# Joints of an eight-norm trunk in float32: six output tiles side by side, and VectorE alone for the sums

## The chip, the core and the metric

The kernel runs on one core of a Trainium2 chip. The metric is the device time of one execution in microseconds (us); lower is better. The engines are TensorE (PE, the matrix products; PEld its weight loads), VectorE (DVE), ScalarE (ACT), GpSimd (POOL) and SyncE (SP, which issues the weight loads).

## What is computed

A trunk of two layers on 272 tokens (16 learned ones and 256 of the input) by 1024 features, all in float32. Each layer has three sublayers: a feed-forward part, a mixer (a gated short convolution in layer 0, differential attention with 8 heads in layer 1), and a second feed-forward part. Each sublayer is normed on its way in and on its way out:

```python
def rms_norm(t, g, eps=1e-6):
    return t * rsqrt(mean(t * t, axis=-1) + eps) * g

def swiglu(h, w_gu, w_down):                     # 1024 -> 2 x 2816 -> 1024
    g, u = split(h @ w_gu, 2, axis=-1)
    return (silu(g) * u) @ w_down

for i in range(2):
    f = swiglu(rms_norm(h, ln_ffn1[i, 0]), ffn1_w_gu[i], ffn1_w_down[i])
    h = h + 0.5 * rms_norm(f, ln_ffn1[i, 1])
    m = mixer(rms_norm(h, ln_mix[i, 0]))         # 1024 -> 3072 -> 1024
    h = h + rms_norm(m, ln_mix[i, 1])
    f = swiglu(rms_norm(h, ln_ffn2[i, 0]), ffn2_w_gu[i], ffn2_w_down[i])
    h = h + 0.5 * rms_norm(f, ln_ffn2[i, 1])
return h[:, 16:]
```

## The kernel before

Activations lie transposed, 128 features by 272 tokens a tile, eight tiles (k = 0 to 7) for 1024 features. From the attention's queries on, 256 tokens are enough. Every weight tile of 128x128 and every activation tile is split into two float32r parts, hi and lo, that add up to it: ScalarE casts the upper part (L138, L212) and VectorE subtracts (L140, L213). A product is then three matmuls: hi by hi, hi by lo of x, lo by hi (`mm3`, L164 to L166).

Weights come as loads of 1 MB with 16 tiles each into three buffers. `prepare` splits a *group* of 8 tiles into one of `HIS = 7` pairs of buffers, about four groups ahead of TensorE; it does so when the program comes to certain tiles of the stream. TensorE's instructions have the order of the program; those of the other engines are ordered by a scheduler.

The sublayers are called f0, cv (convolution), f1, f2, at (attention) and f3. Between one's last down-projection tile and the next one's up-projection lies a *joint*:

- `Post.root`: the mean of the squares of the eight output tiles, as matmuls with a matrix of ones (`ms_out`, L287), the root on ScalarE (`sz`, L313), and ten products that nothing reads (`warm_a`, `warm_b`).
- `Pre.first`: x for k = 0. The residual h and the output f have been multiplied by the gain on GpSimd; VectorE then does hg * s (L379) and the sum, written as x's upper part (L380); GpSimd does the same sum in full (L381), and VectorE takes the lower part from it (L384).
- `Post.z` for k = 1 to 7 on VectorE: t = h * s (L321), z = t + f (L323); `split` with the gain: ScalarE hi (L212), VectorE lo (L213).
- the squares of z on ScalarE (`sq_in`), summed up on GpSimd (`acc_in`, L271).

Since a projection is linear, the norm ahead of it is not applied to x; its factor is put on the output. So TensorE can start on k = 0 at once: `order_up` takes the first `KO = 4` output tiles k by k, tiles 0 to 31 in the order of use, and all others one after the other. At tile `LATE = 40` the mean `ms_in` is formed, from the sum split into hi and lo; then come root and reciprocal (`rs`), and only then are output tiles taken from their PSUM banks, of which there are eight. At this place the residual is brought back, too: h = z / s, a reciprocal on VectorE (`rho`, L330) and eight products on GpSimd (L334).

In attention, the rotation of q and k ends on GpSimd (`rot_q`, `rot_k`, `q`, `k`, L529 and L530), and head 0's scores are put ahead of tile 62 or later (`t0 + 6`), each further part of a head at its own tile.

The functions that the change touches, with the lines of the profile:

## Time and profile before

| | |
|---|---|
| median of 3 runs | 1080.92 us (1080.53 to 1081.65) |
| the profiled execution's span (its own time, first to last instruction) | 1078.5 us |
| PE busy | 1042.0 us, 97% |
| DVE / ACT / POOL busy | 739.5 / 562.5 / 273.0 us |
| weights and inputs read | 174.08 MB, 162 GB/s over the span |

The median is 2.4 us above the span of the profiled execution; no row shows what lies in between. Matmuls are pipelined, so the 0.29 us of a matmul's record are no step; the step is the distance between two starts. A row gives its start, its duration, engine, line, tiles written and read, and in brackets the idle time ahead of it and what ended it. L numbers are lines of the kernel before.

### The profile page before, as it was taken

Reading aid. Unit: us, or ns where it says so; the run is one execution under the profiler, and the core shown is the slowest. Engines: PE = TensorE matmul, PEld = TensorE weight load, DVE = VectorE, ACT = ScalarE, POOL = GpSimd, SP = SyncE. Lnnn points to the kernel's source line nnn. Section 1 sums busy time; section 2 is a strip of 40 time slices with the busy share of each in tenths; the row PEclk is TensorE's granted clock in tenths of the full one; section 3 lists DMA queues with packets and bytes.
Section 4 is the critical chain, followed back from the end, with each engine's and each line's share of the span. In section 5 each row is a group of like instructions: output and inputs, shape, how many; then the busy total and the mean of one; then the engine's idle time right before and its main releaser. Section 6 shows DMA issues by size and latency. Waiting matters only on the chain.

```text
span 1078.5 us, 20013 instructions
## 1 busy us (share of the span) xinstructions
PE 1042.0 (97%) x7948; PEld 1009.6 (94%) x7948; DVE 739.5 (69%) x1379; ACT 562.5 (52%) x1231; POOL 273.0 (25%) x285
## 2 busy tenths in 40 slices
PE   8999999999999999999899999998899989999997
PEld 7999999899989999999799999997889979999986
DVE  6966654498749966644598665438999879866543
ACT  7744444355546644445366444445466656655542
POOL 4211110161137211110363111105612135211000
PEclk9999999999999999999999999999899999999999
DMA  7755445326532754444137545450344413745541
GB/s 272 260 192 174 179 171 182 118 79 234 196 118 78 261 189 176 171 182 160 75 123 274 191 162 191 157 195 5 114 157 157 153 43 131 286 177 190 176 156 40
DMA packets 26878, 176.41 MB, mean 164 GB/s; under 512 B 3104, under 2 KB 4256, under 8 KB 6048
## 3 DMA queue, kind: packets, MB, share of 16 engines
q1 hardware_dynamic: 26640, 175.08, 45.1%
q8 instruction: 62, 1.02, 0.4%
q14 instruction: 32, 0.26, 0.1%
q10 hardware_dynamic: 144, 0.06, 0.0%
HBM read 174.08 MB, written 1.05 MB: 162 GB/s over the span
## 4 chain that ended last, share of the span: by engine, by line
PE 83%; DVE 11%; issue 2%; ACT 2%; POOL 1%; DMA 0%; SPq 0%; DVEq 0%; POOLq 0%
PE ps_guf L166 14%; PE ps_guf L164 14%; PE ps_guf L165 14%; PE ps_dnf L164 6%; PE ps_dnf L166 6%; PE ps_dnf L165 6%; PE ps_cin L166 2%; PE ps_out L697 2%; PE ps_out L695 2%; PE ps_out L696 2%; PE ps_cin L165 2%; PE ps_cin L164 2%; DVE lo_guf L140 1%; PE ps_qkv L164 1%; PE ps_qkv L166 1%
## 5 line engine op out<-in xcount | busy, mean ns | idle before, releaser
L165 PE MATMUL ps_guf<-x_f_lo,hi_guf 128*128 128x272 f32 (+1 forms) x1392 | 400.2, 288 | 4.3 <-DVE x_f_lo L213 4.3
L164 PE MATMUL ps_guf<-x_f_hi,hi_guf 128*128 128x272 f32 (+1 forms) x1392 | 400.7, 288 | 1.7 <-ACT hi_guf L138 1.7
L166 PE MATMUL ps_guf<-x_f_hi,lo_guf 128*128 128x272 f32 (+1 forms) x1392 | 401.1, 288 | 1.1 <-DVE lo_guf L140 1.1
L138 ACT CAST hi_guf<-raw_guf 128x512 fp32r<-128x512 f32 x352 | 199.6, 617 | 142.6 <-PE ps_guf L165 65.4
L165 PEld LDWEIGHTS ps_guf<-x_f_lo,hi_guf 128*128 128x128 f32 x1392 | 265.3, 191 | 5.3 <-DVE x_f_lo L213 4.9
L164 PEld LDWEIGHTS ps_guf<-x_f_hi,hi_guf 128*128 128x128 f32 x1392 | 263.4, 189 | 2.0 <-ACT hi_guf L138 1.9
L166 PEld LDWEIGHTS ps_guf<-x_f_hi,lo_guf 128*128 128x128 f32 x1392 | 263.0, 189 | 1.7 <-DVE lo_guf L140 1.7
L140 DVE TENSOR_TENSOR lo_guf<-raw_guf,hi_guf 128x512 fp32r<-128x512 f32 x352 | 243.8, 733 | 27.0 <-ACT hi_guf L138 19.7
L423 POOL TENSOR_TENSOR sg_f<-sg_f,rs_f 128x272 f32<-128x272 f32 (+1 forms) x88 | 95.8, 1092 | 356.9 <-ACT sg_f L422 356.8
L140 DVE TENSOR_TENSOR lo_dnf<-raw_dnf,hi_dnf 128x512 fp32r<-128x512 f32 x176 | 114.8, 692 | 101.5 <-ACT hi_dnf L138 99.1
L138 ACT CAST hi_dnf<-raw_dnf 128x512 fp32r<-128x512 f32 x176 | 100.8, 619 | 129.5 <-PE ps_dnf L165 50.6
L164 PE MATMUL ps_dnf<-a_f_hi,hi_dnf 128*128 128x272 f32 x528 | 152.2, 288 | 0.0
L166 PE MATMUL ps_dnf<-a_f_hi,lo_dnf 128*128 128x272 f32 x528 | 152.1, 288 | 0.0
L165 PE MATMUL ps_dnf<-a_f_lo,hi_dnf 128*128 128x272 f32 x528 | 151.7, 287 | 0.0
L165 PEld LDWEIGHTS ps_dnf<-a_f_lo,hi_dnf 128*128 128x128 f32 x528 | 100.0, 189 | 0.0
L164 PEld LDWEIGHTS ps_dnf<-a_f_hi,hi_dnf 128*128 128x128 f32 x528 | 99.4, 188 | 0.0
L166 PEld LDWEIGHTS ps_dnf<-a_f_hi,lo_dnf 128*128 128x128 f32 x528 | 99.2, 188 | 0.0
L428 DVE TENSOR_TENSOR av_f<-ps_guf,sg_f 128x272 f32<-128x272 f32 (+1 forms) x88 | 38.3, 436 | 75.7 <-PE ps_guf L166 61.7
L420 DVE TENSOR_TENSOR g_f<-ps_guf,rs_f 128x272 f32<-128x272 f32 (+1 forms) x88 | 37.4, 432 | 39.1 <-PE ps_guf L166 39.1
L271 POOL TENSOR_TENSOR acc_out_f<-acc_out_f,sq_out_f 128x272 f32<-128x272 f32 x21 | 18.0, 859 | 159.3 <-ACT sq_out_f L269 159.3
L166 PE MATMUL ps_qkv<-x_at_hi,lo_qkv 128*128 128x272 f32 (+1 forms) x188 | 55.3, 294 | 3.0 <-DVE lo_qkv L140 3.0
L164 PE MATMUL ps_qkv<-x_at_hi,hi_qkv 128*128 128x272 f32 (+1 forms) x188 | 57.2, 304 | 0.0
(303 smaller groups left out, 1725.4 us busy)
## 6 DMA issues: line engine op xcount, KB each, us to landing
raw_guf<-in_guf SPq DMA_DIRECT2D x86, 1024.0 KB, 4.8
raw_dnf<-in_dnf SPq DMA_DIRECT2D x44, 1024.0 KB, 4.8
raw_cin<-in_cin SPq DMA_DIRECT2D x12, 1024.0 KB, 4.8
raw_qkv<-in_qkv SPq DMA_DIRECT2D x12, 1024.0 KB, 4.8
raw_cout<-in_cout SPq DMA_DIRECT2D x4, 1024.0 KB, 4.8
raw_o<-in_o SPq DMA_DIRECT2D x4, 1024.0 KB, 4.8
raw_guf<-in_guf SPq DMA_DIRECT2D x8, 256.0 KB, 4.9
h<-in_xT SPq DMA_DIRECT2D x8, 136.0 KB, 4.7
```

The costliest lines, as they stand in the source:

```text
L138: nc.scalar.copy(hi[:, sl], both[:, sl])
L140: nc.vector.tensor_tensor(lo[:, sl], both[:, sl], hi.bitcast(F32)[:, sl], ALU.subtract)
L164: nc.tensor.matmul(o, whi, xhi, start=start, stop=False)
L165: nc.tensor.matmul(o, whi, xlo, start=False, stop=False)
L166: nc.tensor.matmul(o, wlo, xhi, start=False, stop=stop)
L271: self.eng.tensor_tensor(self.acc[:, :n], self.acc[:, :n], sq[:, :n], ALU.add)
L420: nc.vector.tensor_tensor(g[:, :n], p, pre.r, ALU.mult)
L423: nc.gpsimd.tensor_tensor(s[:, :n], s[:, :n], pre.r, ALU.mult)
L428: nc.vector.tensor_tensor(v[:, :n], p, keep.pop(j)[:, :n], ALU.mult)
L695: nc.tensor.matmul(o, xhi[:, tok], whi[:, col], start=k == 0, stop=False)
L696: nc.tensor.matmul(o, xhi[:, tok], wlo[:, col], start=False, stop=False)
L697: nc.tensor.matmul(o, xlo[:, tok], whi[:, col], start=False, stop=k == KF - 1)
```

## The change

`KO` is six and `LATE` is 50: six output tiles run k by k (tiles 0 to 47). In each of these eight k steps TensorE does all six hi-by-hi products first, then the six with the weights' lower part, then the six with x's lower part; before, only k = 0 was done so. GpSimd has no instruction in a joint: VectorE does t, z, x's lower part and the sum of the squares for each k. For k = 0 the gain is put into the first six weight tiles instead of into x (`GAINS`), so that z itself goes to TensorE. The orders of VectorE and ScalarE in the joint are those of the program. The mean `ms_in` is one float32 matmul on the sum. Groups are prepared at k = 2, 6 and 7 of a joint, and two more of them in the last 16 tiles of the stream ahead, so that all seven buffers are filled when a joint begins. The residual h is formed at tile 74 instead of 40, and the attention's heads are 10 tiles later at most. At the start (f0, without a joint) the weights come in pieces of six tiles, VectorE does the sum, and the root's table is loaded first.

```diff
-LATE_AT = (30, 34)
+MORE_AT = (2, 6, 7)
+FIRST_AT = (0, 1, 3, 4, 5, 7)
...
-KO = 4
-LATE = KO * KD + 8
+KO = 6
+LATE = KO * KD + 2
...
+        gain = GAINS[label][:, 0:1] if label in LATER and c == g == 0 else None
+        for s, e in ((0, 4), (4, 8)) if gain is None else ((0, KO), (KO, HC)):
+            sl = slice(s * P, e * P)
+            if gain is None or s:
+                with queued(last["sqrt"]):
+                    nc.scalar.copy(hi[:, sl], both[:, sl])
+                with queued(last["rs"]):
+                    nc.vector.tensor_tensor(lo[:, sl], both[:, sl], hi.bitcast(F32)[:, sl], ALU.subtract)
+            else:
+                nc.scalar.activation(hi[:, sl], both[:, sl], AF.Copy, scale=gain)
+                nc.vector.scalar_tensor_tensor(lo[:, sl], both[:, sl], gain, hi.bitcast(F32)[:, sl], ALU.mult, ALU.subtract)
...
+            if pre is not None:
+                pre.before(i)
+            if label in (*LATER, "guf0") and i <= LATE:
+                pass
+            elif j == HC // 2:
                 prepare()
...
+            elif j == 2 and (i > len(order) - 2 * HC and after.get(label) in LATER or ahead(label, i) < AHEAD):
                 prepare()
             hi, lo = group(label, i)
...
+            xhi, xlo = pre.x0 if pre is not None and i < KO else xs[k]
             x0 = c0 if xhi.shape[1] == T else 0
             args = open_[m][:, :n], whi, wlo, xhi[:, x0 : x0 + n], xlo[:, x0 : x0 + n], count[m] == 0, count[m] == nk - 1
-            if before is None or i >= KO:
+            if pre is None or i >= KO * KD:
                 mm3(*args)
             else:
                 held.append(args)
-                if i == KO - 1:
-                    for o, hi, lo, xhi, xlo, start, _ in held:
+                if len(held) == KO:
+                    for o, hi, lo, xhi, xlo, start, stop in held:
                         nc.tensor.matmul(o, hi, xhi, start=start, stop=False)
-                    for o, hi, lo, xhi, xlo, start, _ in held:
+                    for o, hi, lo, xhi, xlo, start, stop in held:
                         nc.tensor.matmul(o, lo, xhi, start=False, stop=False)
-                    for o, hi, lo, xhi, xlo, start, _ in held:
-                        nc.tensor.matmul(o, hi, xlo, start=False, stop=False)
+                    for o, hi, lo, xhi, xlo, start, stop in held:
+                        nc.tensor.matmul(o, hi, xlo, start=False, stop=stop)
+                    held.clear()
...
+            if self.extra is not None and self.i == 1:
+                nc.vector.scalar_tensor_tensor(self.acc[:, :n], self.extra, EPS * D / P, sq[:, :n], ALU.mult, ALU.add)
+            elif self.i < KD or not self.soon:
                 self.eng.tensor_tensor(self.acc[:, :n], self.acc[:, :n], sq[:, :n], ALU.add)
             else:
                 self.last = sq
...
+            parts = [self.acc, self.last] if self.soon else [self.acc]
+            for i, t in enumerate(parts):
+                nc.tensor.matmul(o, ones, t[:, :n], start=i == 0, stop=i == len(parts) - 1)
...
+        def z(self, hk, k, hi=None):
             n = self.n
             t = tmp.tile([P, T], F32, tag="t", bufs=3, name=f"t_{self.name}_{k}")
-            with queued(self.after):
-                nc.vector.tensor_tensor(t[:, :n], hk[:, self.c0 - (T - hk.shape[1]) :], self.s[:, :n], ALU.mult)
+            nc.vector.tensor_tensor(t[:, :n], hk[:, self.c0 - (T - hk.shape[1]) :], self.s[:, :n], ALU.mult)
             z = self.f[k]
-            self.after = nc.vector.tensor_tensor(z, t[:, :n], self.f[k], ALU.add)
+            if hi is not None:
+                nc.vector.tensor_tensor(hi, t[:, :n], z, ALU.add)
+            nc.vector.tensor_tensor(z, t[:, :n], z, ALU.add)
             return z
...
+            k, j = divmod(i, KO)
+            if i < KD * KO and j == 0:
+                if k == 0:
+                    self.order = ExitStack()
+                    self.order.enter_context(tc.manual_schedule(engines={mybir.EngineType.DVE, mybir.EngineType.Activation}))
+                if self.post is None:
+                    if k == 0:
+                        self.zs = self.hs
+                        self.norm = Norm(f"in_{self.name}", self.n, eng=nc.vector, soon=False)
+                        for e in range(2):
+                            self.part(e)
+                            prepare()
+                        self.x0 = self.xs[0]
+                    if k + 2 < KD:
+                        self.part(k + 2)
+                    if k in FIRST_AT:
+                        prepare()
+                    self.norm.add(self.zs[k])
+                else:
+                    if k == 0:
+                        self.first()
+                        self.step(1)
+                    if k < KD - 1:
+                        self.step(k + 2)
+                    for _ in range(MORE_AT.count(k)):
+                        prepare()
             if i == LATE:
                 self.ms = self.norm.mean()
                 self.ready()
+                self.order.close()
+            if i == LATE + 3 * KD:
+                self.residual()
+            self.parts(i)
...
+            n, post = self.n, self.post
             post.root()
...
+            hi = tmp.tile([P, n], F32R, tag="zh0", bufs=1, name=f"z_{self.name}_0_hi")
+            lo = tmp.tile([P, n], F32R, tag="zl0", bufs=1, name=f"z_{self.name}_0_lo")
+            z = self.zs[0] = post.z(self.hs[0], 0, hi)
+            nc.vector.tensor_tensor(lo, z, hi.bitcast(F32), ALU.subtract)
+            self.x0 = hi, lo
+            self.zs[1] = post.z(self.hs[1], 1)
+            self.norm = Norm(f"in_{self.name}", n, post.ms, nc.vector, soon=False)
+        def step(self, k):
+            if k + 1 < KD:
+                self.zs[k + 1] = self.post.z(self.hs[k + 1], k + 1)
+            if k < KD:
+                self.part(k)
+            if k == KD:
+                self.norm.add(self.zs[k - 1])
+                self.part(0)
+            else:
+                self.norm.add(self.zs[k - 1])
...
-            t0 = max(3 * KD * (hd + 1), 56 + 10 * hd)
+            t0 = max(3 * KD * (hd + 1), LATE + 16 + 10 * hd)
```

How the instructions move, at three places. ScalarE at the end of f0's down projection and the begin of the joint to cv, first before, then after; `sq_out_f` is the square of an output tile, `hi_cin` a group's upper part (x2: two halves), `sz_f` the root:

```order
L138 CAST hi_cin_1_2598<-raw_cin_2566 128x512 x2
L269 ACTIVATE sq_out_f_7_2524<-ps_dnf_6_2443 128x272
L304 ACTIVATE f_f_6_2527<-ps_dnf_6_2443,half_112 128x272
L269 ACTIVATE sq_out_f_8_2616<-ps_dnf_7_2529 128x272
L304 ACTIVATE f_f_7_2618<-ps_dnf_7_2529,half_112 128x272
L313 ACTIVATE sz_f_2634<-ms_out_f_2631 128x272
```

```order
L289 ACTIVATE sq_out_f_7_2529<-ps_dnf_6_2448 128x272
L319 ACTIVATE f_f_6_2532<-ps_dnf_6_2448,half_115 128x272
L144 CAST hi_cin_0_2581<-raw_cin_2579 128x512 x2
L144 CAST hi_cin_1_2605<-raw_cin_2579 128x512 x2
L144 CAST hi_cin_0_2619<-raw_cin_2617 128x512 x2
L289 ACTIVATE sq_out_f_8_2637<-ps_dnf_7_2534 128x272
L319 ACTIVATE f_f_7_2639<-ps_dnf_7_2534,half_115 128x272
L328 ACTIVATE sz_f_2650<-ms_out_f_2647 128x272
```

Three groups more stand between the last square but one and the last; the third takes the seventh pair of buffers. VectorE from the root on in the same joint, before and after:

```order
L379 TENSOR_TENSOR hg_cv<-hg_cv,sz_f_2634 128x272
L380 TENSOR_TENSOR x_cv_hi<-hg_cv,fg_cv 128x272
L321 TENSOR_TENSOR t_f_1_2648<-h_79,sz_f_2634 128x272
L323 TENSOR_TENSOR f_f_1_2068<-t_f_1_2648,f_f_1_2068 128x272
L384 TENSOR_TENSOR x_cv_lo<-x_cv,x_cv_hi 128x272
L321 TENSOR_TENSOR t_f_2_2687<-h_80,sz_f_2634 128x272
L213 SCALAR_TENSOR_TENSOR x_cv_lo<-f_f_1_2068,gains,x_cv_hi 128x272
L323 TENSOR_TENSOR f_f_2_2160<-t_f_2_2687,f_f_2_2160 128x272
```

```order
L334 TENSOR_TENSOR t_f_0_2663<-h_78,sz_f_2650 128x272
L337 TENSOR_TENSOR z_cv_hi<-t_f_0_2663,f_f_0_1987 128x272
L338 TENSOR_TENSOR f_f_0_1987<-t_f_0_2663,f_f_0_1987 128x272
L411 TENSOR_TENSOR z_cv_lo<-f_f_0_1987,z_cv_hi 128x272
L334 TENSOR_TENSOR t_f_1_2668<-h_79,sz_f_2650 128x272
L338 TENSOR_TENSOR f_f_1_2073<-t_f_1_2668,f_f_1_2073 128x272
L334 TENSOR_TENSOR t_f_2_2672<-h_80,sz_f_2650 128x272
L338 TENSOR_TENSOR f_f_2_2167<-t_f_2_2672,f_f_2_2167 128x272
L231 SCALAR_TENSOR_TENSOR x_cv_lo<-f_f_1_2073,gains,x_cv_hi 128x272
L291 SCALAR_TENSOR_TENSOR acc_in_cv<-ms_out_f_2647,sq_in_cv_2679 128x272
```

The full sum of k = 0 is now VectorE's, its lower part comes right after it, and each k ends with a sum of squares. GpSimd in attention, from the residual to head 1's q, before and after (`h_f` is the residual; in each list the first `rot_q`, `rot_k`, `q`, `k` are head 0's):

```order
L334 TENSOR_TENSOR h_f_6_9275<-f_f_6_8864,rho_f_9261 128x272
L334 TENSOR_TENSOR h_f_7_9277<-f_f_7_8957,rho_f_9261 128x272
L376 TENSOR_SCALAR hg_f_10855<-h_f_0_9263,gains 128x256
L529 TENSOR_TENSOR rot_q_9283<-rot_q_9283,sr 128x256
L529 TENSOR_TENSOR rot_k_9289<-rot_k_9289,sr 128x272
L529 TENSOR_TENSOR rot_q_9297<-rot_q_9297,sr 128x256
L530 TENSOR_TENSOR q_9285<-q_9285,rot_q_9283 128x256
L530 TENSOR_TENSOR k_9291<-k_9291,rot_k_9289 128x272
```

```order
L349 TENSOR_TENSOR h_f_3_9483<-f_f_3_8600,rho_f_9475 128x272
L562 TENSOR_TENSOR rot_q_9299<-rot_q_9299,sr 128x256
L562 TENSOR_TENSOR rot_k_9305<-rot_k_9305,sr 128x272
L563 TENSOR_TENSOR q_9301<-q_9301,rot_q_9299 128x256
L562 TENSOR_TENSOR rot_q_9313<-rot_q_9313,sr 128x256
L349 TENSOR_TENSOR h_f_4_9485<-f_f_4_8694,rho_f_9475 128x272
L563 TENSOR_TENSOR k_9307<-k_9307,rot_k_9305 128x272
L349 TENSOR_TENSOR h_f_5_9487<-f_f_5_8780,rho_f_9475 128x272
L349 TENSOR_TENSOR h_f_6_9489<-f_f_6_8873,rho_f_9475 128x272
L349 TENSOR_TENSOR h_f_7_9491<-f_f_7_8980,rho_f_9475 128x272
L563 TENSOR_TENSOR q_9315<-q_9315,rot_q_9313 128x256
```

The residual's eight products, which were all done before the first rotation, now lie among those of heads 0 and 1.

## Rows read from the trace of the kernel before

**Rows 1.** The page: busy time of TensorE, and the chain that ended last, by engine.

```profile
PE 1042.0 (97%) x7948; PEld 1009.6 (94%) x7948; DVE 739.5 (69%) x1379; ACT 562.5 (52%) x1231; POOL 273.0 (25%) x285
PE 83%; DVE 11%; issue 2%; ACT 2%; POOL 1%; DMA 0%; SPq 0%; DVEq 0%; POOLq 0%
```

**Rows 2.** Timeline (start, duration, instruction, idle before) of TensorE, joint f0 to cv.

```profile
208.14 0.29 PE L166 MATMUL ps_dnf<-a_f_hi,lo_dnf 128*128 128x272 f32 x1
...
211.80 0.77 PE L190 MATMUL ps_cin<-x_cv_hi,hi_cin 128*128 128x272 f32 x4 [1.22 <-DVE x_cv_hi L380]
...
214.01 0.77 PE L194 MATMUL ps_cin<-x_cv_lo,hi_cin 128*128 128x272 f32 x4 [0.93 <-DVE x_cv_lo L384]
...
221.68 0.39 PE L165 MATMUL ps_cin<-x_cv_lo,hi_cin 128*128 128x272 f32 x1 [1.81 <-DVE x_cv_lo L213]
...
232.52 0.29 PE L164 MATMUL ps_cin<-x_cv_hi,hi_cin 128*128 128x272 f32 x1
```

**Rows 3.** Stretches (length, busy per engine, PEclk, DMA): joints (f1's left out), half clock, steady work.

```profile
208.14:232.52 24.38, 20.41 (x139) 18.84 (x138) 21.91 (x32) 13.94 (x31) 14.83 (x17) 0.93 0.02 4
...
522.75:547.12 24.37, 19.11 (x139) 17.35 (x138) 21.89 (x32) 13.94 (x31) 14.81 (x17) 1.00 0.03 4
730.65:755.00 24.35, 20.35 (x139) 18.54 (x138) 21.90 (x36) 13.95 (x31) 14.54 (x16) 0.93 0.04 5
873.22:897.60 24.38, 19.71 (x140) 18.13 (x139) 21.85 (x35) 14.91 (x36) 14.07 (x16) 0.93 0.03 5
744.40:747.90 3.50, 3.50 (x18) 3.50 (x18) 3.29 (x8) 2.12 (x6) 1.75 (x3) 0.51 0.00 0
40.00:200.00 160.00, 160.00 (x1277) 160.00 (x1276) 95.65 (x171) 79.87 (x161) 24.88 (x25) 1.00 0.53 189
```

**Rows 4.** Timeline of VectorE in the joint to cv.

```profile
210.17 0.44 DVE L379 TENSOR_TENSOR hg_cv<-hg_cv,sz_f 128x272 f32<-128x272 f32 x1 [8.90 <-ACT sz_f L313]
210.72 1.03 DVE L380 TENSOR_TENSOR x_cv_hi<-hg_cv,fg_cv 128x272 fp32r<-128x272 f32 x1
...
214.99 0.43 DVE L321 TENSOR_TENSOR t_f<-h,sz_f 128x272 f32<-128x272 f32 x1
215.45 0.44 DVE L323 TENSOR_TENSOR f_f<-t_f,f_f 128x272 f32<-128x272 f32 x1
215.81 0.50 DVE L213 SCALAR_TENSOR_TENSOR x_cv_lo<-f_f,gains,x_cv_hi 128x272 fp32r<-128x272 f32 x1
...
225.35 1.84 DVE L330 RECIPROCAL rho_f<-sz_f 128x272 f32<-128x272 f32 x1
```

**Rows 5.** Timeline of GpSimd: joint to cv, and the residual in attention.

```profile
210.69 0.76 POOL L381 TENSOR_TENSOR x_cv<-hg_cv,fg_cv 128x272 f32<-128x272 f32 x1 [8.79 <-DVE hg_cv L379]
...
749.76 8.69 POOL L334 TENSOR_TENSOR h_f<-f_f,rho_f 128x272 f32<-128x272 f32 x8 [1.21 <-DVE rho_f L330]
```

**Rows 6.** Timeline of ScalarE: the last square, the root, casts of two groups.

```profile
208.53 0.40 ACT L269 ACTIVATE sq_out_f<-ps_dnf 128x272 f32<-128x272 f32 x1 [7.39 <-PE ps_dnf L166]
...
209.74 0.40 ACT L313 ACTIVATE sz_f<-ms_out_f 128x272 f32<-128x272 f32 x1 [0.44 <-PE ms_out_f L287]
...
224.87 2.16 ACT L138 CAST hi_cin<-raw_cin 128x512 fp32r<-128x512 f32 x4
```

**Rows 7.** Timeline of TensorE: attention up to head 0's scores, and f3's first products.

```profile
765.81 0.59 PE L166 MATMUL ps_qkv<-x_at_hi,lo_qkv 128*128 128x272 f32 x1 [3.03 <-DVE lo_qkv L140]
...
767.02 1.31 PE L549 MATMUL pss<-k,q 64*128 64x144 f32 x6
...
877.31 0.74 PE L190 MATMUL ps_guf<-x_f_hi,hi_guf 128*128 128x256 f32 x4 [0.59 <-DVE x_f_hi L380]
```

**Rows 8.** A wait of the start (who waited for whom: total us, times, longest).

```profile
PE ps_guf L164 <- ACT hi_guf L138: 1.7, 1, 1.7
```

**Rows 9.** Timeline of ScalarE at the start: the first two casts of weights.

```profile
4.62 0.62 ACT L138 CAST hi_guf<-raw_guf 128x512 fp32r<-128x512 f32 x1 [0.77 <-DMA raw_guf<-in_guf]
...
7.01 0.62 ACT L138 CAST hi_guf<-raw_guf 128x512 fp32r<-128x512 f32 x1 [0.65 <-DMA raw_guf<-in_guf]
```

More of the change, by code (lines that the diff above doesn't have):

```diff
@@ L145, in group, with ahead, stream @@
         return groups[label, c, j // HC]
-    def stream(label):
+    def ahead(label, i):
+        done, c = len(groups) - base[label], i // HC
+        return done - c - 1
+    base, taken = {}, 0
+    for label, n in n_groups.items():
+        base[label] = taken
+        taken += n
+    def stream(label, pre=None):
         order = a["streams"][label][1]
         for i, km in enumerate(order):
-            c, j = divmod(i, CH)
-            g, j = divmod(j, HC)
-            if (label, c, g) not in groups:
+            j = i % HC
+            if pre is not None:
[3 more added lines that the diff above has]
+            elif j == HC // 2:
                 prepare()
-            if label in LATER and i < KD * KO:
-                for _ in range(LATE_AT.count(i)):
-                    prepare(after=True)
-            elif j == HC // 2:
+            elif j == 2 and (i > len(order) - 2 * HC and after.get(label) in LATER or ahead(label, i) < AHEAD):
                 prepare()
@@ L328, in h @@
             r = tmp.tile([P, T], F32, tag="rho", bufs=1, name=f"rho_{self.name}")
-            with queued(last["lo"]):
+            with queued(last["rs"]):
                 nc.vector.reciprocal(r[:, :n], self.s[:, :n])
@@ L412, in ready @@
             table(AF.Silu, s)
-            pre.residual()
         pre.ready = ready
```

114 lines of the change are left out of this document (30 added, 84 removed).

## The prediction

> **What bounds the kernel now.** I read the page first: TensorE is busy 97% of the span and 83% of the chain that ended last, so what the change can win is time in which TensorE stands still or has too little ready [rows 1]. Then TensorE's timeline at one joint. Between f0's last down product (208.14) and cv's tile 40 (232.52) it stands 1.22 us for x's upper part of k = 0, 0.93 us for its lower part and 1.81 us for a later lower part, and each time the releaser is VectorE [rows 2]. Then the stretches: the joints take 24.35 to 24.38 us each (four rows; f1's reads as cv's), and in steady work 1277 products take 160.0 us, 0.125 us each, 0.375 us per tile of three products [rows 3]. Forty tiles are 15.0 us, so each joint loses 9.4 us. VectorE is busy for 21.9 of the 24.4 us with 32 instructions, 0.68 us each: it is the bound of the joint [rows 3]. Last I looked at what makes its instructions long. The sum of 128x272 at 210.72 took 1.03 us, while GpSimd did a sum at 210.69 [rows 4, 5]; with GpSimd quiet, t, z and the lower part took 0.43, 0.44 and 0.50 us, with 0.46, 0.36 and about 0.4 us from start to start [rows 4].
>
> The Trainium skill, page "SBUF — State Buffer", section "Who interferes with whom", says that a VectorE instruction with two inputs in SBUF contends with a GpSimd instruction that reads SBUF, and one of them blocks. The rows on the joint agree (1.03 against 0.44 us). By that rule removing GpSimd gives all VectorE instructions of the joint the short time; nothing below needs it.
>
> A drop of the granted clock is in these stretches, too: cv's, at's and f3's joints show 0.93 on average (f1's too), f2's shows 1.00, and all take the same time [rows 3]. So half clock costs nothing in a joint as it is; TensorE would have waited for VectorE anyway. One such stretch (3.5 us at 0.51, the lower of the clock's two levels, 1.2 of 2.4 GHz) does half the work [rows 3]; where TensorE is the bound it costs 1.7 us.
>
> **The change part by part.** I count from the last down product to tile 50, where the mean is now formed. Before: 24.38 + 10 x 0.375 = 28.1 us.
>
> *Start of a joint.* Before, the first product of cv comes 211.80 - 208.14 = 3.66 us after the last [rows 2]. The chain in between is square (208.53), mean, root (209.74), hg * s (210.17), sum (210.72, 1.03 us) [rows 4, 6]. The sum alone now takes 0.44 to 0.5: -0.55 us. Against that, ScalarE now has three groups of casts ahead of the last square. The third takes the seventh pair of buffers, which comes free only when TensorE is nearly through with the stream: its cast waits for the last product but one with that pair, and the square, the root and all upper parts are queued behind. Two casts are 2 x 0.54 = 1.08 us (four took 2.16) [rows 6]. I reckon that they begin about 0.1 us before the square was due: the square comes 0.96 us later. Bounds: 0 if the pair is free earlier, 2 us if two groups come late. Start: 3.66 - 0.55 + 0.96 = 4.07 us.
>
> *The k steps.* TensorE needs 18 products per k, 2.25 us. VectorE has t, z, a lower part and a sum per k: 0.46 + 0.36 + 0.42 + about 0.4 = 1.65 us; the sum is not in the trace on VectorE, and I take the time of z. Eight k are 13.2 us; with two more instructions for k = 0 (0.9) and six half groups (0.36 x 512 / 272 = 0.68 each, an estimate from z; 4.1) it's 18.2 us in 40 instructions, and VectorE starts 1 us ahead of TensorE, which needs 50 x 0.375 = 18.75 us. So VectorE is ahead by about 1.5 us at the end, more in the middle, and TensorE is the bound. ScalarE has a square (0.40) and an upper part (I take 0.54, a cast's) per k and six casts, 11 us, and is far ahead [rows 6]. GpSimd has nothing.
>
> *The mean.* One float32 product instead of two of float32r. The `ms_out` products are of that kind; between square (208.53 + 0.40) and root (209.74) lies one, 0.5 us with the ways to and from it [rows 6]. Tile 50 lies at 4.07 + 0.2 (for the first products to get going) + 18.75 + 0.5 = 23.5 us: **4.6 us won in each of cv, f1 and f2, 13.8 us**. What comes late next: the bank of the first output tile is wanted at tile 64, 14 x 0.375 = 5.2 us after tile 50; Root (0.40) and reciprocal (1.84) leave 3 us for VectorE to get to the first reading [rows 4, 6], and I take that as enough. If not, it costs up to 2 us a joint.
>
> *f3.* Two groups of casts stand among its squares (+2.16); before, the first product came at 877.31 - 873.22 = 4.09 [rows 3, 7], now 5.7. With 256 columns a tile is 0.353 (by the columns): 5.7 + 0.2 + 17.65 + 0.5 = 24.1 against 24.38 + 3.53 = 27.9: 3.8 us. TensorE has then stood almost 6 us with only the ten warming products, and I count one stretch of half clock: **2.1 us won** (bounds 0 and 4).
>
> *Attention.* Up to tile 50 as the others, 4.6 us. Then the residual's eight products, 1.09 us each (8.69 for eight) [rows 5], no longer lie ahead of the heads but among them, and the reciprocal for them stands on VectorE ahead of the rotations. Head 0's k is the tenth thing that GpSimd does after the residual's reciprocal, with five residuals (5.4) and five instructions of 0.76 (as the sum in [rows 5]) before or in it, 9.2 us; root and two reciprocals (0.40 + 2 x 1.84) [rows 4, 6] stand ahead: about 13.5 us after tile 50. Its scores are wanted at tile 72, 8.2 us after tile 50: a new wait of about 5.4 us, behind which TensorE's further tiles queue. Before, TensorE stood 3.03 us at 765.81 for a lower part and came to the scores (tile 62) at 767.02, 36.4 us after its last product, at half clock [rows 3, 7]; tile 72 lay 1.3 + 10 x 0.375 + about 2 for the clock further on, at 43.5. After: 23.5 + 22 x 0.375 + 5.4 + 1.3 = 38.4. That is 5 us won, less a stretch of half clock after the wait (1.7) and about 1.8 for the later turn of head 0, whose w comes later: **1.5 us** (bounds -3 and 5).
>
> *Start.* TensorE's wait of 1.7 us goes, for its cast stood behind one that waited for GpSimd's sum, and the sum is VectorE's now [rows 8]. But the first six tiles need the fourth load, not the second: 392 KB took 7.01 - 4.62 = 2.4 us [rows 9], so the fourth, with 256 KB more ahead than what had come by 7.01, lands near 8.6, and TensorE stands for it. **0.5 us won** (bounds -2 and 2).
>
> *The clock in the other four joints.* TensorE's idle time at the start is 0.4 us longer and all other is gone; I count 1 us in all.
>
> *Cost at nothing.* The residual in the feed-forward joints (tile 74): GpSimd is held for 8.7 us [rows 5], the gated product behind it waits, and TensorE has some 25 tiles (9.4 us) of other work before it needs that tile's bank; without this cover it would cost a few us a joint. The gain on the first weights: in the stream before, where VectorE is busy for 96 of 160 us and ScalarE for 80 [rows 3].
>
> Sum: 13.8 + 2.1 + 1.5 + 0.5 - 1.0 = 16.9 us. From the profiled span, 1078.5, this makes 1061.6; the median lies 2.4 above that span, so **1064.0 us** stands against 1080.92.
>
> **Rivals.**
>
> *A, all covers hold.* The casts do not hold up the square (0.96 x 4 + 2.16), attention keeps its 5 us (3.5) and no half clock (2.7): 12.2 us more, 1052. For it: ScalarE had been idle 7.39 us ahead of the last square [rows 6]. Against it: the seventh pair can't be free before TensorE has left it.
>
> *B, the clock.* What was hidden [rows 3] is now paid: a stretch of half clock in each joint and two in attention, 6 x 1.7 = 10.2 instead of the 2.7 and 1.7 counted, with a bank late in one joint: 1071. For it: a longer stand at the begin of each joint. Against: f2's joint, with all of its stands, kept 1.00.
>
> The Trainium skill, page "TensorE: Matmul & The Clock Gate", section "Part 1: The HAM clock gate (the "warmup" mystery)", says that the gate goes by how busy TensorE has been recently. By that rule the long stands at 219 to 222 and in its like are what calls the drops before, and a joint without them has fewer; f2's joint doesn't bear it out as a certainty.
>
> *C, slower: VectorE is the bound alone.* It takes over the sums, 40 instructions in a joint. If they take 0.68 us each as in the joint before [rows 3], it needs 40 x 0.23 = 9.2 us more than reckoned, 1.5 of them hidden: 7.7 - 4.6 = 3.1 us slower than before in each joint, 15 in all, 1096. It decides from 0.60 us an instruction. For it: the written order lets VectorE stop for each of ScalarE's answers. Against: without GpSimd at work, rows show 0.36 to 0.46 from start to start [rows 4].
>
> *D, no change.* TensorE's waits move and don't shrink: VectorE near 0.60 us, 1081.
>
> **Chances and range.** Forecast 0.56, A 0.12, B 0.18, C 0.10, D 0.04. A measurement of this kernel tells 0.2% (2.2 us) from no change. Faster: forecast, A and B, 0.86; within 0.2%: D, 0.04; slower: C, 0.10. The range for 8 in 10 goes from 1054 (part of A; f3 and attention at their better bounds) to 1075 (B with one more bank late); C lies outside.
>
> **What would show it.** Five joints of about 23.5 us to tile 50 (f3 24.1), TensorE without a wait of over 0.3 us between k = 1 and k = 7; VectorE at 0.45 us an instruction with 128x272; the last square about 1 us later behind two casts; a wait of about 5 us ahead of head 0's scores, on GpSimd. I am wrong if TensorE waits for lower parts inside the k steps, if the granted clock stays at half for more than 3.5 us in a feed-forward joint, or if TensorE waits at tile 64.

## The result, and the profile after

The changed kernel takes 1066.84 us (1065.28 to 1067.72, 4 runs) against 1081.29 us of the kernel before on the same chip: a ratio of 0.9865, with a 95% interval of 0.9851 to 0.9879. The prediction said 1064.0 us, 1054 to 1075, faster.

The profiled execution has a span of 1063.5 us, 15.0 less than before (1078.5). Cut at the last down product of each sublayer, which each trace gives to 0.01 us, this is where it comes from:

| from one last product to the next | before | after | won | forecast |
|---|---|---|---|---|
| start and f0 | 208.14 | 209.84 | -1.70 | 0.5 |
| cv | 106.71 | 102.87 | 3.84 | 4.6 |
| f1 | 207.90 | 203.10 | 4.80 | 4.6 |
| f2 | 207.89 | 203.09 | 4.80 | 4.6 |
| at | 142.57 | 142.35 | 0.22 | 1.5 |
| f3 to the end | 205.24 | 202.25 | 2.99 | 2.1 |

The last column leaves out the 1.0 us that was counted for the clock in four joints together. Line numbers from here on are those of the changed kernel (and may differ by one in an experiment).

The page of the changed kernel, the two lines that answer to [rows 1]: TensorE carries 88% of the chain that ended last instead of 83, VectorE 6 instead of 11, and GpSimd has lost 74 us of work.

```profile
PE 1035.5 (97%) x7948; PEld 1005.5 (95%) x7948; DVE 722.8 (68%) x1427; ACT 560.8 (53%) x1229; POOL 199.2 (19%) x211
PE 88%; DVE 6%; ACT 2%; POOL 1%; issue 1%; DMA 0%; SPq 0%; DVEq 0%; POOLq 0%
```

The stretches that answer to [rows 3], from the last down product to tile 50 in each joint (length, busy time per engine with instructions, granted clock, DMA). Before, tile 50 came 28.1 us after the last product; now it is 23.15, with 42 instructions of VectorE in 18.43 us, 0.44 us each instead of 0.68, and with GpSimd idle but for one memset. The clock is 1.00 in four of five joints; f3's has 0.93.

```profile
209.84:232.99 23.15, 21.88 (x169) 20.80 (x168) 18.43 (x42) 11.84 (x27) 0.32 (x1) 1.00 0.31 111
312.71:335.87 23.16, 21.89 (x170) 20.81 (x168) 18.43 (x42) 11.84 (x27) 0.32 (x1) 1.00 0.32 110
515.81:538.96 23.15, 21.88 (x170) 20.80 (x168) 18.43 (x42) 11.84 (x27) 0.32 (x1) 1.00 0.33 110
718.90:741.64 22.74, 21.47 (x169) 20.33 (x168) 19.73 (x49) 11.84 (x27) 0.00 (x0) 1.00 0.30 104
861.25:886.78 25.53, 22.07 (x170) 20.86 (x168) 20.24 (x47) 13.86 (x34) 0.00 (x0) 0.93 0.30 107
```

The begin of the joint to cv on TensorE, against [rows 2], and on ScalarE, against [rows 6]. Two casts wait for TensorE's end and stand before the square, which comes at 211.09, 1.25 us after the last product instead of 0.39 [rows 2, 6]; TensorE waits 0.70 us for it behind the first half of the mean. The first product starts 3.85 us after the last (213.69 against 209.84), and no other wait of TensorE follows in this joint.

```profile
209.84 0.29 PE L185 MATMUL ps_dnf<-a_f_hi,lo_dnf 128*128 128x272 f32 x1
...
211.53 0.73 PE L302 MATMUL ms_out_f<-sq_out_f,ones 128*128 128x272 f32 x2 [0.70 <-ACT sq_out_f L289]
212.09 1.04 PE L103 MATMUL warm_b_f<-warmer 128*128 128x256 bf16 x8
213.69 1.02 PE L207 MATMUL ps_cin<-z_cv_hi,hi_cin 128*128 128x272 f32 x6 [0.56 <-DVE z_cv_hi L337]
```

```profile
210.04 1.14 ACT L144 CAST hi_cin<-raw_cin 128x512 fp32r<-128x512 f32 x2 [1.86 <-PE ps_dnf L184]
211.09 0.39 ACT L289 ACTIVATE sq_out_f<-ps_dnf 128x272 f32<-128x272 f32 x1
```

VectorE in one k of the same joint, against [rows 4]: t, z, lower part and sum take 1.59 us from one t to the next.

```profile
216.93 0.43 DVE L334 TENSOR_TENSOR t_f<-h,sz_f 128x272 f32<-128x272 f32 x1
217.39 0.44 DVE L338 TENSOR_TENSOR f_f<-t_f,f_f 128x272 f32<-128x272 f32 x1
217.75 0.49 DVE L231 SCALAR_TENSOR_TENSOR x_cv_lo<-f_f,gains,x_cv_hi 128x272 fp32r<-128x272 f32 x1
218.17 0.43 DVE L293 TENSOR_TENSOR acc_in_cv<-acc_in_cv,sq_in_cv 128x272 f32<-128x272 f32 x1
218.52 0.43 DVE L334 TENSOR_TENSOR t_f<-h,sz_f 128x272 f32<-128x272 f32 x1
```

### The profile page after: what moved, and what is told of

The parts are those of the page before. It is cut to its first block, busy times and chain, and to the rows that moved or that the text cites. A ratio compares the mean times of both kernels' runs of the same rounds, so it can differ in the third digit from the quotient of the medians.

```text
span 1063.5 us, 19962 instructions
## 1 busy us (share of the span) xinstructions
PE 1035.5 (97%) x7948; PEld 1005.5 (95%) x7948; DVE 722.8 (68%) x1427; ACT 560.8 (53%) x1229; POOL 199.2 (19%) x211
## 4 chain that ended last, share of the span: by engine, by line
PE 88%; DVE 6%; ACT 2%; POOL 1%; issue 1%; DMA 0%; SPq 0%; DVEq 0%; POOLq 0%
PE ps_guf L185 14%; PE ps_guf L183 14%; PE ps_guf L184 14%; PE ps_dnf L183 6%; PE ps_dnf L184 6%; PE ps_dnf L185 6%; PE ps_guf L207 2%; PE ps_guf L209 2%; PE ps_guf L211 2%; PE ps_out L727 2%; PE ps_out L725 2%; PE ps_out L726 2%; PE ps_qkv L183 1%; DVE lo_cin L146 1%; PE ps_qkv L184 1%
## 5 line engine op out<-in xcount | busy, mean ns | idle before, releaser
L185 PE MATMUL ps_guf<-x_f_hi,lo_guf 128*128 128x272 f32 (+1 forms) x1216 | 349.0, 287 | 0.6 <-DVE lo_guf L146 0.6
L183 PE MATMUL ps_guf<-x_f_hi,hi_guf 128*128 128x272 f32 (+1 forms) x1216 | 349.4, 287 | 0.0
L184 PE MATMUL ps_guf<-x_f_lo,hi_guf 128*128 128x272 f32 (+1 forms) x1216 | 347.6, 286 | 0.0
L146 DVE TENSOR_TENSOR lo_guf<-raw_guf,hi_guf 128x512 fp32r<-128x512 f32 x349 | 236.7, 717 | 31.9 <-ACT hi_guf L144 25.9
L184 PEld LDWEIGHTS ps_guf<-x_f_lo,hi_guf 128*128 128x128 f32 x1216 | 230.7, 190 | 0.1
L185 PEld LDWEIGHTS ps_guf<-x_f_hi,lo_guf 128*128 128x128 f32 x1216 | 228.5, 188 | 0.8 <-DVE lo_guf L146 0.8
L183 PEld LDWEIGHTS ps_guf<-x_f_hi,hi_guf 128*128 128x128 f32 x1216 | 228.8, 188 | 0.1
L458 POOL TENSOR_TENSOR sg_f<-sg_f,rs_f 128x272 f32<-128x272 f32 (+1 forms) x88 | 91.9, 1048 | 454.9 <-ACT sg_f L457 454.9
L227 ACT CAST a_f_hi<-av_f 128x272 fp32r<-128x272 f32 (+1 forms) x88 | 36.4, 414 | 33.0 <-DVE av_f L463 32.9
L457 ACT ACTIVATE sg_f<-g_f 128x272 f32<-128x272 f32 (+1 forms) x88 | 36.8, 424 | 19.8 <-DVE g_f L455 19.8
```

Of the source, the lines that this page charges most:

```text
L146: nc.vector.tensor_tensor(lo[:, sl], both[:, sl], hi.bitcast(F32)[:, sl], ALU.subtract)
L183: nc.tensor.matmul(o, whi, xhi, start=start, stop=False)
L184: nc.tensor.matmul(o, whi, xlo, start=False, stop=False)
L185: nc.tensor.matmul(o, wlo, xhi, start=False, stop=stop)
L227: nc.scalar.copy(hi, x)
L457: nc.scalar.activation(s[:, :n], g[:, :n], AF.Silu)
```

## Experiments

Times are medians on the chip; "joint" means the time from a last down product to the mean's product (`ms_in`, just ahead of tile 50), read at f0 to cv: 22.9 us in the changed kernel.

**Four tiles again.**

```diff
-KO = 6
-LATE = KO * KD + 2
+KO = 4
+LATE = 50
```

> Four output tiles side by side again (KO = 4, the mean still at tile 50), all else as changed: VectorE alone, written order. Theory 1 (both parts are needed, but the short VectorE instructions carry most): TensorE now has only 1.5 us of products per k, VectorE needs 1.58 us and three pairs of splits, so TensorE waits for it; x's last lower part comes 16.8 us after the last down product, tile 50 at about 24.8 us instead of 23.2 (28.1 before): 1.6 us a joint, 8 us in all, 1075 us. Theory 2 (it is the six tiles side by side that cover VectorE; GpSimd's absence does little): the joint falls back to about 28 us to tile 50, 1088 to 1091 us. In either case VectorE's instructions of 128x272 stay at 0.36 to 0.48 us from start to start.

Measured: 1078.0 us (0.9968, 0.9955 to 0.9981 of before), joint 24.94. Theory 1's mechanism holds, and its size is a little under the measured one (tile 50 comes at 25.2 us, forecast 24.8): TensorE waits for an upper and for a lower part inside the k steps (waits: who for whom, us in total, times, longest).

```profile
PE ps_cin L211 <- DVE x_cv_lo L231: 1.0, 1, 1.0
...
PE ps_cin L207 <- ACT x_cv_hi L230: 0.6, 1, 0.6
```

The time is 3 us over theory 1's. By the profile each joint costs 2.0 us instead of 1.6, the start and f0 are 1.3 us longer (211.16; KO changes the order of the start, too), and cv loses 1.5 us more than its joint: from 296 to 299 us the granted clock is 0.50.

**GpSimd's sums back.**

```diff
-            self.norm = Norm(f"in_{self.name}", n, post.ms, nc.vector, soon=False)
+            self.norm = Norm(f"in_{self.name}", n, post.ms, nc.gpsimd, soon=False)
```

> The sums of squares in the joint go back to GpSimd (seven of the eight; the first stays on VectorE), all else as changed, six tiles side by side. Theory 1 (contention makes VectorE's instructions long): those of VectorE with two inputs in SBUF that overlap one of GpSimd's seven sums take 0.85 to 1.0 us again; VectorE has one instruction per k fewer and needs 1.7 to 2.2 us per k, still under TensorE's 2.25: the time stays within 2 us of the changed kernel (1065 to 1069). Theory 2 (GpSimd's absence is what brings the gain): VectorE needs over 2.3 us per k, TensorE waits for lower parts, 2 to 4 us a joint, 1077 to 1087 us. Theory 3 (no contention; the long instructions of before had another cause): VectorE's instructions stay at 0.43 to 0.5 us and the time is the same.

Measured: 1066.98 us, joint 22.9: the same. Theory 1 held, and VectorE's rows show the contention. The sum z at 217.99 and the lower part at 220.05 lie beside GpSimd's sums at 217.81 and 219.91 and take twice as long; those between don't.

```profile
217.53 0.43 DVE L334 TENSOR_TENSOR t_f<-h,sz_f 128x272 f32<-128x272 f32 x1
217.99 0.90 DVE L338 TENSOR_TENSOR f_f<-t_f,f_f 128x272 f32<-128x272 f32 x1
218.81 0.49 DVE L231 SCALAR_TENSOR_TENSOR x_cv_lo<-f_f,gains,x_cv_hi 128x272 fp32r<-128x272 f32 x1
...
220.05 1.01 DVE L231 SCALAR_TENSOR_TENSOR x_cv_lo<-f_f,gains,x_cv_hi 128x272 fp32r<-128x272 f32 x1
```

```profile
217.81 0.78 POOL L293 TENSOR_TENSOR acc_in_cv<-acc_in_cv,sq_in_cv 128x272 f32<-128x272 f32 x1 [6.00 <-ACT sq_in_cv L289]
219.91 0.85 POOL L293 TENSOR_TENSOR acc_in_cv<-acc_in_cv,sq_in_cv 128x272 f32<-128x272 f32 x1 [1.32 <-ACT sq_in_cv L289]
```

So with six tiles side by side VectorE has room for these longer instructions.

**Both at once** (the two edits above).

> Four output tiles side by side, and the sums of squares on GpSimd (the fourth corner beside the changed kernel, KO = 4 alone and GpSimd's sums alone). Theory (with four tiles VectorE is the bound of the joint, so every instruction that GpSimd lengthens counts; with six it does not): VectorE has one instruction fewer per k (0.4 us) and two that take 0.45 us more, so x's last lower part comes 1.5 to 2 us later than with KO = 4 alone: the mean 26.4 to 27 us after the last down product instead of 24.9, 1084 to 1088 us. Rival (GpSimd's part costs nothing with four tiles either): 1076 to 1080 us as with KO = 4 alone.

Measured: 1083.58 us (1.0019, 1.0010 to 1.0028 of before: slower), joint 26.06. The mechanism is the theory's, the size a little under it: with four tiles GpSimd's sums cost 1.1 us a joint, with six nothing.

**Six tiles and nothing else**, in the kernel before.

```diff
-KO = 4
-LATE = KO * KD + 8
+KO = 6
+LATE = KO * KD + 2
...
-LATE_AT = (30, 34)
+LATE_AT = (13, 19, 25, 31)
```

> The kernel before with six output tiles side by side and the mean at tile 50, and nothing else of the change: GpSimd still works in the joints, the scheduler orders VectorE and ScalarE; groups of weights are prepared at tiles 13, 19, 25 and 31 of a joint instead of 30 and 34, since 48 tiles are wanted. Theory (the six tiles are what carries the gain): VectorE's last lower part came 17 us after the last down product, TensorE gets there at 20; TensorE waits for the first lower part only (0.9 us), and the joint takes 24.4 to 25 us to tile 50 instead of 28.1: 3 to 3.7 us a joint, 1064 to 1069 us. Rival (without VectorE alone and the written order TensorE still waits for lower parts, or VectorE's splits of the groups come between): 26.5 us or more to tile 50, 1073 to 1081 us.

Measured: 1097.12 us (1.0142, 1.0124 to 1.0160 of before: slower), joint 27.0. The rival was right on the joint, and the time is 16 us over its worst case. The waits of TensorE in and after the joint to cv (lines of the kernel before):

```profile
PE ps_cin L164 <- DVE c L455: 3.4, 1, 3.4
PE ps_cin L165 <- DVE x_cv_lo L213: 2.4, 3, 1.6
PE ps_cin L190 <- DVE x_cv_hi L380: 1.2, 1, 1.2
PE ps_cin L194 <- DVE x_cv_lo L384: 0.4, 1, 0.4
```

VectorE's splits of weights, long beside GpSimd, stand ahead of lower parts:

```profile
218.12 2.43 DVE L140 TENSOR_TENSOR lo_cin<-raw_cin,hi_cin 128x512 fp32r<-128x512 f32 x2
220.47 0.99 DVE L213 SCALAR_TENSOR_TENSOR x_cv_lo<-f_f,gains,x_cv_hi 128x272 fp32r<-128x272 f32 x1
221.39 1.85 DVE L140 TENSOR_TENSOR lo_cin<-raw_cin,hi_cin 128x512 fp32r<-128x512 f32 x2
```

The 3.4 us are the wait for a bank that the prediction named as a danger at tile 64: VectorE comes to the first output tile too late. In the three feed-forward parts such waits take 8.7 us, and head 0's scores wait 6.8 us for GpSimd's k. The changed kernel has none of these bank waits in cv or in the feed-forward parts. This run also prepares four groups inside the joint, so it does not show six tiles with the splits of weights elsewhere.

**The scheduler's order in the joints.**

```diff
-                    self.order.enter_context(tc.manual_schedule(engines={mybir.EngineType.DVE, mybir.EngineType.Activation}))
+                    pass
```

> The written order of VectorE and ScalarE in the joints is given up; the scheduler orders them, all else as changed (six tiles side by side, no GpSimd in the joint). Theory (with 2.25 us of products per k the order hardly matters, VectorE has 3 us to spare at the end of a joint): within 2 us of the changed kernel, 1065 to 1069. Rival (the written order is what keeps each lower part in time; the scheduler puts casts and splits of weights, or all t and z, ahead of lower parts): TensorE waits 1 to 3 us in each joint, 1072 to 1082 us.

Measured: 1065.99 us, joint 23.07: 0.17 us a joint more, and the same time. With six tiles and GpSimd out of the joint the written order is worth next to nothing; with four tiles it was not tried.

**The last square first.**

```diff
-MORE_AT = (2, 6, 7)
+MORE_AT = (1, 2, 6, 7)
...
             elif j == HC // 2:
-                prepare()
+                if after.get(label) not in LATER or i < len(order) - HC:
+                    prepare()
```

> The last group that is prepared ahead of a joint (the one that takes the seventh pair of buffers) is prepared at k = 1 of the joint instead, so that no cast that waits for TensorE's end stands ahead of the last square. Theory (the casts hold up the square, 1.09 us a joint, and 1.1 of f3's two): the first product comes 2.8 us after the last down product instead of 3.85, cv, f1, f2 and at win 1.05 us each and f3 1.1: 1061.5 us. Rival (the first product is set by something else: the sum of squares on GpSimd, or the group at k = 1 comes too late for tile 48): the square moves up but the time stays, 1066 to 1068, or TensorE waits inside the joint for a weight tile.

Measured: 1059.17 us (0.9791, 0.9777 to 0.9806 of before), joint 21.99: 7.7 us less than the changed kernel. The square follows the last product (209.28) at once, and the first product comes after 2.94 us instead of 3.85 (a row of ScalarE, one of TensorE):

```profile
209.61 0.40 ACT L290 ACTIVATE sq_out_f<-ps_dnf 128x272 f32<-128x272 f32 x1 [1.99 <-PE ps_dnf L186]
```

```profile
212.22 1.02 PE L208 MATMUL ps_cin<-z_cv_hi,hi_cin 128*128 128x272 f32 x6 [0.57 <-DVE z_cv_hi L338]
```

In the profiles cv, f1, f2 and at win 0.9 us each and f3's stretch 2.1, 5.7 in all; f3's joint has the clock at 1.00 here, 0.93 in the changed kernel. The start is 0.6 us shorter. The rest of the 7.7 us lies between medians and profiled executions: the one of the changed kernel was its fastest run (1065.28 us).

**Attention's residual late, by its place in the program.**

```diff
-            if i == LATE + 3 * KD:
+            if i == (len(ORD_QKV) - 2 if self.name == "at" else LATE + 3 * KD):
                 self.residual()
```

> In attention alone, the residual h (a reciprocal on VectorE, eight products on GpSimd) moves from tile 74 to tile 190, behind the last head's rotations. Theory (these products stand between head 0's rotations and make TensorE wait, 1.4 + 2.6 + 0.8 + 3.7 us, and the half clock after two of these waits takes 3 us more): head 0's k is ready 5 us earlier, the waits ahead of the scores go, that ahead of w's transposes shrinks; 4 to 8 us won, 1059 to 1063 us. Rival (attention is bound by VectorE up to its last heads, so what is won at head 0 is lost behind): the early waits shrink, others come up later, attention keeps its 142 us, 1066 to 1068 us.

Measured: 1067.41 us, and the same waits. But this run tests neither forecast: `residual` asks for its reciprocal right behind the norm's, the products need nothing else, and the scheduler leaves both where they were, whatever tile the program names.

**Attention's residual late, by the instruction it follows.** As above, and:

```diff
-            with queued(last["rs"]):
+            with queued(last["rot"] if self.name == "f2" else last["rs"]):
                 nc.vector.reciprocal(r[:, :n], self.s[:, :n])
...
-            nc.vector.tensor_tensor(q[:, :n], p, cr[:, c0:], ALU.mult)
+            last["rot"] = nc.vector.tensor_tensor(q[:, :n], p, cr[:, c0:], ALU.mult)
```

> In attention alone, the reciprocal of the residual is put behind the last head's k on VectorE by name, so that the eight products on GpSimd follow head 7's rotations (moving it in the program alone, in the run before, left both engines' orders as they were). Theory (these products and their reciprocal hold up heads 0 and 1): the waits of 1.55 us at tile 64 and 2.7 us at head 0's scores go, that of 3.9 us ahead of w's transposes shrinks, the stretch of half clock behind goes: attention takes 136 to 139 us instead of 142.4, 1060 to 1063 us. Rival (VectorE is the bound through the heads): the early waits go, as much waiting comes up later, attention stays within 1 us of 142.4.

Measured: 1064.5 us (0.9848, 0.9832 to 0.9864 of before), attention 140.5 us instead of 142.4. The early waits are gone, and one wait of 5.5 us ahead of w's transposes has taken their place:

```profile
PE pw L619 <- DVE w L606: 5.5, 1, 5.5
```

Attention wins 1.9 us of some 8 us of waiting: more than the rival's 1 us, and less than the theory's 3.4 to 6.4. Most of what was won early is lost again at w.

**The start's loads cut at 8, 12, 20, 24, 32, 36, 44 and 48 tiles.**

```diff
-        i, end = k * KO, (k + 1) * KO
+        i, end = (0, 8, 12, 20, 24, 32, 36, 44, 48)[k : k + 2]
```

> Only the loads of the start are cut otherwise: 8 tiles first, then up to tile 12, 20, 24, 32, 36, 44, 48, so that the first six tiles are there with the first weight load and not with the second. Theory (the second load, which the fourth to sixth tile waited for, sets the start): TensorE's first six products begin 0.9 us after one another's data, at about 6.7 and 7.2 us, without the gap of 1 to 2.3 us behind the fourth product; f0's last product comes 0.5 to 1.5 us earlier. Rival (the start is held by the lower clock: after the warming products TensorE stands for a us, and products are 0.227 us apart up to 13 us): the gap goes but the clock stays low as long, gain under 0.5 us.

Measured: 1063.64 us (0.9847, 0.9832 to 0.9862 of before); f0's last product at 206.53 instead of 209.84. More than either forecast; the stretches show why (6 to 13 us: the changed kernel, the one before, this run).

```profile
6.00:13.00 7.00, 6.21 (x26) 5.90 (x27) 5.59 (x11) 5.45 (x13) 0.00 (x0) 1.00 1.04 373
```

```profile
6.00:13.00 7.00, 6.79 (x48) 6.53 (x48) 5.34 (x9) 6.33 (x15) 4.47 (x5) 1.00 1.00 331
```

```profile
6.00:13.00 7.00, 6.59 (x52) 6.59 (x53) 5.37 (x10) 5.15 (x11) 0.00 (x0) 1.00 1.02 358
```

26 products in 7 us, against 48 and 52. The 26 that this run has more of are 3.25 us of work at 0.125 us each, and 3.3 us is what f0's last product gains.

**And 30 warming products ahead.** As above, and `START_WARM = 30` instead of 18.

> As the run with other pieces at the start, and 30 warming products ahead instead of 18, so that TensorE has work up to the first real product. Theory (the clock): products are 0.125 us apart from about 7 us on instead of 13, f0's last product comes 2 to 3.5 us earlier than with the pieces alone, 1062 to 1064 us. Rival (the clock's level at the start is not set by that stand): same as the run with the pieces alone, or later by what the products cost.

Measured: 1063.26 us, f0's last product at 206.44: the same as with the pieces alone, as the rival had it. But with the pieces alone the products have full pace from the first one on (first starts 6.41 and 6.64, then 0.124 to 0.14 us apart), although TensorE had stood for 1.2 us ahead of it; so there was nothing left for the warming products to win.

**The three that helped, together** (the last square first; pieces and 30 warming products; the residual behind the heads).

> The changed kernel with the three edits that helped: the last square ahead of the casts, the start's loads cut at 8, 12, 20 and so on with 30 warming products, and the residual of attention behind the heads. Theory (the gains are in different places and add up): against the changed kernel 7.7 + 3.5 + 2.3 = 13.5 us less, 1052 to 1055 us. Rival (part of it was the same time counted twice, the clock's above all): 1056 to 1060 us.

Measured: 1056.08 us (0.9761, 0.9744 to 0.9777 of before), 10.8 us less than the changed kernel and the fastest of all. By parts they would have been 13.6. The profiles place 2.3 of the missing 2.8 us: cv takes 103.44 us here and 101.92 in the run with the last square first alone, f3's stretch 201.00 and 200.18. In both places the granted clock is at half for a while, where that run has 1.00:

```profile
288.00:292.00 4.00, 4.00 (x22) 4.00 (x21) 1.38 (x2) 1.36 (x4) 0.97 (x1) 0.57 0.18 57
858.00:862.00 4.00, 3.86 (x21) 3.24 (x20) 3.55 (x10) 1.27 (x4) 0.00 (x0) 0.57 0.32 133
```

So the rival's range was met, and its clock is where most of the difference lies.

**Head 0's transposes later.** On top of the last:

```diff
-(heads[hd].turn, 24), (heads[hd].values, 32)
+(heads[hd].turn, 24 if hd else 38), (heads[hd].values, 32 if hd else 46)
```

> The run with the three edits together, and head 0's transposes of w and its values 14 tiles later (38 and 46 tiles after its place instead of 24 and 32). What is open is whether attention's remaining wait (5.5 us ahead of these transposes) is a matter of place or of VectorE's work. Theory (place: w comes late only for head 0, TensorE has other tiles to do): the wait goes, and the half clock behind it, 1049 to 1052 us. Rival (VectorE is the bound through the heads): TensorE waits elsewhere for as long, for w of head 1 or for a bank, 1055 to 1058 us.

Measured: 1057.13 us, as the rival had it: the wait comes some 5 us later and is 5.9 us instead of 5.5 (waits of TensorE in attention, then the stretch of 737 to 800 us).

```profile
PE pw L620 <- DVE w L607: 5.9, 1, 5.9
```

```profile
737.00:800.00 63.00, 57.08 (x428) 51.36 (x429) 58.91 (x169) 37.85 (x120) 21.11 (x24) 0.95 0.33 119
```

VectorE is busy for 58.9 of 63 us there, and for 58.5 in the run with the three edits together, so where the transposes stand makes no difference. That VectorE is the bound of attention's first heads is read from this; no run made its work there shorter.

## Why the prediction was right, and where not

The time lies 2.8 us above the forecast and well inside its range, but part of that closeness is luck: by the table, the start (2.2 us), attention (1.3) and cv (0.8) came out worse, f3 (0.9), the clock (1.0) and f1 and f2 (0.4) better.

*What bounds the joint* was right, and the runs show how the two parts belong together. Joints by number of tiles and by who does the sums, with all other edits in place: four and GpSimd 26.06, four and VectorE 24.94, six and GpSimd 22.9, six and VectorE 22.9. The kernel before stands at 27.9 (tile 50 at 28.1, less the 0.26 us from mean to tile 50), and with six tiles alone at 27.0. Six tiles alone win 0.9 us in the joint and lose more behind it; everything but six tiles wins 2.9; both win 5.0. TensorE's work per k must be longer than VectorE's (2.25 against 1.59 us now), and that took a shorter VectorE as well as a longer TensorE. The prediction had put the two into one sum and so couldn't say which carries it. Of the 2.9 us the sums of squares are 1.1; the rest was not taken apart.

*Start of a joint*: 4.07 us forecast, 3.85 measured. The new wait behind ScalarE's casts was forecast at 0.96 us a joint; the square came 0.86 us later than before, and taking the casts away gave 0.9 in cv, f1, f2 and at. This cost stood inside the forecast gain, and a kernel without it is 7.7 us faster.

*The k steps and the mean*: TensorE had no wait between k = 1 and k = 7, tile 50 at 23.15 against 23.5 forecast. VectorE's instructions took 0.44 us (0.45 forecast), and it had more to spare than the 1.5 us: its last lower part is done at 227.9, 4.8 us ahead of the mean's product, and four of the six half groups of weights are split behind it. f1 and f2 won 4.8 against 4.6.

*Convolution*, 3.84 of 4.6: a wait that the prediction didn't have. TensorE, now earlier, gets to the output projection before its last input. The waits, and VectorE ahead of them: splits of weights stand between the convolution's own steps.

```profile
PE ps_cout L183 <- ACT a_cv_hi L227: 0.8, 1, 0.8
PE ps_cout L184 <- DVE a_cv_lo L228: 0.7, 1, 0.7
```

```profile
286.16 1.28 DVE L146 TENSOR_TENSOR lo_cout<-raw_cout,hi_cout 128x512 fp32r<-128x512 f32 x2
287.37 0.49 DVE L496 SCALAR_TENSOR_TENSOR y<-u,gains,y 128x271 f32<-128x271 f32 x1
...
289.35 0.44 DVE L502 TENSOR_TENSOR cv<-ps_cin,y 128x272 f32<-128x272 f32 x1 [0.95 <-POOL y L498]
```

That these splits are the cause is read from the order of the records; no run took them away.

*f3*: the first product came 6.49 us after the last (5.7 forecast), and the granted clock fell after TensorE's stand of 3.5 us. In the stretch from 865 to 869 it is 0.69, a mixture of the two levels. 3.0 us won, with 2.1 forecast, in bounds of 0 and 4. That the clock would fall was no certainty: with the start's loads cut otherwise the same stand of 3.5 us was followed by 1.00 (last line).

```profile
865.22 0.70 PE L302 MATMUL ms_out_at<-acc_out_at,ones 128*128 128x256 f32 x2 [3.46 <-DVE acc_out_at L293]
```

```profile
865.00:869.00 4.00, 3.78 (x18) 2.92 (x19) 2.23 (x7) 0.69 (x2) 0.00 (x0) 0.69 0.44 182
```

```profile
865.00:869.00 4.00, 3.48 (x28) 2.96 (x27) 2.70 (x7) 0.59 (x2) 0.00 (x0) 1.00 0.25 100
```

*Attention*: 0.2 us won instead of 1.5. The sum had one wait of 5.4 us ahead of the scores and 1.8 for the turn; measured were 1.3 us for a bank at tile 64, 2.4 for head 0's k on GpSimd, and 3.6 for w:

```profile
PE pw L619 <- DVE w L606: 3.6, 1, 3.6
PE pss L582 <- POOL k L563: 3.1, 2, 2.4
PE ps_qkv L183 <- DVE q L561: 1.3, 1, 1.3
```

The bank at tile 64 is one of the prediction's own signs of being wrong; it came here and in no other part. The residual's eight products were the cause of the first two waits, 3.7 us, which went when it was moved; that gave 1.9 us, and the rest came back in the third wait. Head 0's scores began 35.2 us after the last product, earlier than the sum's 37.1, so the loss lies behind them. The terms that were mis-sized are "about 1.8 for the later turn of head 0" (a wait of 3.6 us) and one stretch of half clock (two, at 754 and at 771 us). Behind them stands, by its busy time, VectorE's work in the first heads, which the joint's gain doesn't shorten.

*Start*: the step that failed, inside its bounds of -2 and 2. "0.5 us won" was -1.7 in the profile. The wait for a later load was seen, but the sum had TensorE at full pace behind it. Its products are 0.227 us apart up to 13 us (six from 8.68 to 10.04), against the 0.125 of steady work:

```profile
8.68 1.56 PE L209 MATMUL ps_guf<-x_f_hi,lo_guf 128*128 128x272 f32 x6
10.04 1.56 PE L211 MATMUL ps_guf<-x_f_lo,hi_guf 128*128 128x272 f32 x6
```

This is the pace of the clock's lower level. The column PEclk reads 1.00 here only because the trace's record of the clock begins at 13.15 us, when the pace changes. The run that moved attention's residual by its place has the same start, and its record begins earlier: the granted clock is 0.50 there, and the products are as far apart (rows of TensorE, then a stretch).

```profile
9.49 1.56 PE L209 MATMUL ps_guf<-x_f_hi,lo_guf 128*128 128x272 f32 x6
10.85 1.56 PE L211 MATMUL ps_guf<-x_f_lo,hi_guf 128*128 128x272 f32 x6
```

```profile
10.00:14.00 4.00, 4.00 (x19) 4.00 (x19) 3.96 (x8) 3.73 (x9) 0.00 (x0) 0.50 0.86 264
```

All six profiles with six tiles and the start of the changed kernel have products at this pace for 3 to 7 us, somewhere between 6 and 15 us, and TensorE stands for 0.6 to 2.1 us behind the fourth product; in the four with the loads cut otherwise both are gone. That the stand calls the lower level is not shown: in the changed kernel the first four products, ahead of the stand, are slow already, and the two profiles with KO of four have stands of 1.0 to 2.0 us at the start without a drop. f0's last product lies between 209.3 and 211.2 us in the eight profiles that load the start as KO says, KO of four included, and between 206.4 and 206.9 in the other four.

*Rivals.* B's clock did not come: 1 us was counted for the four other joints, and they show 1.00. Before, with stands inside the joints, cv's and at's showed 0.93 [rows 3]; no run tells which stand that hung on. In attention half clock was paid twice, as B had it. The price of such a stretch is a little under the 1.7 us that the prediction took: by 0.227 against 0.125 us a product, the 3.5 us of [rows 3] cost 1.6. C and D are refuted by VectorE's 0.44 us. Of A's 12.2 us the casts' 6.0 came when the casts were moved (5.7 by the profiles); of attention's 3.5, moving the residual gave 1.9. The 3.4 us that the fastest kernel wins at the start are no part of A.

## What to carry to other kernels

Side-by-side work on the engine that should be the bound and shorter work on the engine that feeds it pay together, when the first becomes longer per step than the second; test the two apart and together before giving credit to one. The start lost some 3 us here to a stand and the clock's lower level: look at the distance of products there before reckoning with full pace. When buffers are to be filled before a joint, look at what stands behind the last fill on its engine: an instruction that waits for the end of the stage ahead must come behind the joint's first step. A gain in front of a stage that another engine bounds is lost there, as in attention: find that bound first.
